# The MLP of a decoder layer on one core: single tiles regrouped, and weight sums stored ahead

## The chip, the core and the metric

The kernel runs on one core of one Trainium2 chip. The metric is the device time of one execution in microseconds. A core has five engines that matter here: TensorE for matrix products (its weight loads are shown apart, as PEld, since they overlap the products), VectorE (DVE), ScalarE (ACT), GpSimd (POOL), and SyncE (SP), which here issues the DMA transfers. Each engine works through its own list of instructions in order and waits at an instruction until what that instruction needs is there.

## The reference

One step of a decoder layer with 1032 tokens (a prompt of 1024 and 8 single sample tokens): an input projection, two head groups, an output projection with a layer norm, and then the MLP, which is all that the change touches:

```python
h = jnp.square(jax.nn.relu(jnp.einsum('btd,df->btf', x, w_ff1)))
x = layernorm(DN_ALPHA * x + jnp.einsum('btf,fd->btd', h, w_ff2), ln2_g, ln2_b)
```

D_MODEL is 1024 and the inner width 4096, all in f32. In tiles of 128, the first product makes 32 row tiles of h out of 8 tiles of x; the second makes 8 row tiles of the result, and its sum runs over the 32 tiles of h.

## The kernel before

**Layout and precision.** Tokens are columns: 1032 of them, in two halves of HN = 516, each in two chunks of CH = 258. An f32 operand is split (`split`, L109) into a high part, which ACT makes by a copy (L111), and a low part, which DVE or POOL makes by a subtraction (L112). Each product is then three matmuls: high by high, high by low, low by high. `product` (L1434, the matmul is L1440) runs these over the tiles of the sum, with two matmuls of 128x258 for each, one per chunk, into one PSUM buffer `sb` of two banks; there are four such buffers.

**Pairs.** Both products save matmuls where two output tiles (or two tiles of the sum) are taken together as a pair. The weights of a pair are a block of 2 x 2, A11, A12, A21 and A22, and the two halves of the tokens are the other side. Seven block products, named B21, T1, B11, B22, T2, T3 and T4, take the place of eight. Four of them need sums of the weights: s1 = A21 + A22, s2 = s1 - A11, s4 = A12 - s2 and s3 = A11 - A21. B21 uses A12, T1 uses s1, B11 uses A11, B22 uses s4, T2 uses s2, T3 uses s3 and T4 uses A22. The sides that belong to the tokens ("forms") need sums likewise.

**Where the order comes from.** In the first MLP product, and in what comes before it, TensorE's instructions run in the order in which the program gives them (L1315 sets that for this engine). Everything else, and all of the second product, is put in order by the compiler, which may move an instruction ahead of others. Buffers are another matter: a tile is asked for under a tag with a fixed number of buffers, and the buffers of one tag are handed out in the order in which the program asks for them, each one when the tile that held it before has been read for the last time.

**The first product.** Six of the 32 output tiles (PLAIN, L26: 0, 1, 14, 15, 28, 29) are made singly in an earlier stage (`plain`, L1410). The other 26 are made as 13 pairs in `ff1` (L1541). `pair` (L1455) asks for two tiles of tag `wpair`, which has four buffers of 128x1024 (512 KB), and loads them (L1460): the first holds A11 and A12, the second A21 and A22. The sums go to `wraw` (L1464 to L1467, two buffers; s1 and s4 on DVE, s2 and s3 on POOL). Results are taken out of PSUM into tiles `hst` (four buffers): an addition of two products on DVE (L1483), relu and square on ACT (L1480, L1484, L1485), and a store of h to memory (`hd`, L1486). `minus` (L1489) makes four sums of these outputs per pair, which are forms of the second product, in tiles of tag `hsum` (two buffers of 128x516), on DVE (L1491), and stores them to `ht` (L1492). The first, `minus(0)`, reads the relu of T2 and the result of B11, and stands right behind T2; two come behind T3 and one behind T4.

`pair` is a generator with seven stops. The loop in `ff1` runs the new pair five steps and fits the last two of the pair before it in between, so that TensorE runs B21 of the new pair, T3 of the old, T1 of the new, T4 of the old, and then B11, B22 and T2 of the new.

**The second product.** `ff2` (L1718) goes through the 32 tiles of h in groups (GROUPS, L23): a positive number is that many single tiles, a negative one that many pairs. For each group there are weights laid out by the host as that group needs them (`_layout`, L1804), and forms of h which are loaded and split in preparation (`plain_forms` L1568 with `h_load` L1558, tag `hraw`, two buffers; `pair_forms` L1577, loads L1591 into `hst`, 21 per group of three pairs). The forms live in a ring of 30 slots (RING, L25). A group of single tiles has 16 units (eight output tiles, two halves), a group of three pairs has 4 (`pair_unit`, L1638), each of seven products, of which the last two run beside the next unit. While one group is worked on, the preparation of the next is spread over its units (L1740). `pair_unit` loads the four blocks A of 128x384 (192 KB each) into tag `w2raw`, which has six buffers (WB, L1646), makes s1 to s4 in `wraw` (L1651, on DVE or POOL by the table WE), splits them, and adds each product to the accumulator on DVE (L1668). Where a group of pairs follows a group of single tiles, all its forms go into fresh slots; where it follows pairs, 12 of the 21 can only be made when the old group's slots come free.

The last group (four single tiles) is done by `dense_g` (L1707) together with the closing layer norm (L1773).

Of the kernel before, what the change touches and what calls it, by code (L numbers as in the profile page):

```python
# [9 lines left out]
F32 = mybir.dt.float32  # L10
F32R = mybir.dt.float32r
AF = mybir.ActivationFunctionType
OP = mybir.AluOpType
# [6 lines left out]
LBLK = [(0, 256), (768, 264), (256, 256), (512, 256)]  # L20
PBLK = [(0, 384), (384, 384), (768, 264)]
HN, CH = 516, 258
GROUPS = [2, -3, -3, 2, -3, -3, 4]  # L23
FIRST = [sum(abs(x) * (1 if x > 0 else 2) for x in GROUPS[:g]) for g in range(len(GROUPS))]
RING = "XXLLLLLLQBQBQBQBQBQBQBQQCQCQQB"  # L25
PLAIN = (0, 1, 14, 15, 28, 29)  # L26
PAIRS = [p for p in range(16) if 2 * p not in PLAIN]
FORMS = {"B11": "QL", "B21": "QL", "B12": "XX", "B22": "CL", "T1": "BQ", "T2": "BQ", "T3": "BQ", "T4": "BQ"}
TO = 2
TP = ((1, 3), (0, 1, 3), (0,), (2,))  # L30
LA = (384,384,384,256)
HE = {"B21": 0, "T1": 0, "B11": 0, "B22": 1, "T2": 1, "T3": 0, "T4": 1}
WE = (1, 0, 1, 0, 0, 0, 1, 1, 0, 1, 0)
# [26 lines left out]
class Kernel:  # L60
# [1307 lines left out]
    def out2(self, mixo, acc):  # L1368
        nc = self.nc
        V, G = nc.vector, nc.gpsimd  # L1370
        self.fm = {}
        self.hd = self.dp.tile([32, 128, NT], F32, name="hd", tag="hd")
        self.ht = self.dp.tile([14, 4, 128, HN], F32, name="ht", tag="ht")
        ws = self.resident(self.a["wout"][0], [self.x1slot("wr", w) for w in "LLLLLLBB"], self.tp)

        def units(c0):
            for n_ in range(8):
                ps = self.mmps(CH)
                yield from self.dense_q(ws[n_], mixo, c0, CH, ps)
                V.tensor_tensor(acc[n_][:, c0:c0 + CH], acc[n_][:, c0:c0 + CH], ps, op=OP.add)  # L1380
                yield 3 * CH / 2400.0

        def norm(c, half, fill):
            put = (self.form("B11", c) + self.form("B21", c)) if not half else (self.form("B12", c) + self.form("B22", c))
            for wait in self.layer_norm_x1(acc, HN * half + CH * c, CH, put, LW[2 * c + half]):
                self.ahead(fill, wait)

        order = [(0, 0), (0, 1), (1, 0), (1, 1)]
        us = [units(HN * half + CH * c) for c, half in order]
        self.ahead(us[0], 99)  # L1390
        chain = lambda *gs: (x for g in gs for x in g)
        norm(0, 0, chain(us[1], us[2]))
        self.ahead(us[1], 99)
        norm(0, 1, chain(us[2], us[3]))
        self.ahead(us[2], 99)
        if TO == 0:
            self.t_forms(acc, 0)
        first = self.plain(0)
        norm(1, 0, chain(us[3], first))
        self.ahead(us[3], 99)  # L1400
        if TO == 1:
            self.t_forms(acc, 0)
        norm(1, 1, first)
        if TO == 2:
            self.t_forms(acc, 0)
        self.t_forms(acc, 1)
        self.ahead(first, 999)
        self.ahead(self.plain(1), 999)
# [46 lines left out]
    def pair(self, p):  # L1455
# [82 lines left out]
            out(f + 1, 0, P, m4)  # L1538
        yield

    def ff1(self):  # L1541
        self.ps_ctx.close()
        self.ps_ctx = ExitStack()
        self.sb = self.ps_ctx.enter_context(
            self.tc.tile_pool(name="sb", bufs=4, space=PSUM, reuse_waits="tile"))
        prev = iter(())
        for p in PAIRS:
            cur = self.pair(p)
            for i in range(5):
                next(cur)  # L1550
                if i < 2:
                    next(prev, None)
            prev = cur
        for _ in prev:
            pass
# [12 lines left out]
    def plain_forms(self, g, out):  # L1568
        nc = self.nc
        for j in range(GROUPS[g]):  # L1570
            raw = self.h_load(FIRST[g] + j)
# [5 lines left out]
    def pair_forms(self, g, out):  # L1577
        n = -GROUPS[g]
        slots = {}
        once = GROUPS[g - 1] > 0  # L1580
        early, late = ("B21", "T1", "B11"), ("B22", "T2", "T3", "T4")
# [39 lines left out]
    def plain_units(self, g, hs, acc):  # L1621
        V = self.nc.vector
        nth = sum(1 for x in GROUPS[:g] if x > 0)
        for n_ in range(8):
# [13 lines left out]
    def pair_unit(self, g, q, fs, acc):  # L1638
        nc = self.nc
        V, G = nc.vector, nc.gpsimd  # L1640
        E = lambda i: (V, G)[i]
        n = -128 * GROUPS[g]
        A = {}
        for j in (1, 2, 3, 0):
            A[j] = self.tp.tile([128, 384], F32, name="w2raw", tag="w2raw", bufs=WB)[:, :n]
            nc.sync.dma_start(A[j], self.a["wff2_%d" % g][q][:, n * j:n * j + n])  # L1646
        A11, A12, A21, A22 = (A[j] for j in range(4))

        def add(x, y, op, eng):
            z = self.wp.tile([128, 512], F32, name="wraw", tag="wraw", bufs=2)[:, :n]  # L1650
            eng.tensor_tensor(z, x, y, op=op)  # L1651
            return z
# [18 lines left out]
        product(Q, "B21", A12, E(WE[0]), True, True)  # L1671
        out(0, 0, Q)
        yield
        s1 = add(A21, A22, OP.add, E(WE[1]))
        s2 = add(s1, A11, OP.subtract, E(WE[2]))
        T = self.bank()
        product(T, "T1", s1, E(WE[3]), True)
        out(1, 1, T)
# [2 lines left out]
        product(P, "B11", A11, E(WE[4]), True)  # L1681
        out(0, 0, P)
        yield
        s4 = add(A12, s2, OP.subtract, E(WE[5]))
        product(T, "B22", s4, E(WE[6]), False, True)
        out(0, 1, T)
        yield
        product(P, "T2", s2, E(WE[7]), False)
        out(0, 1, P)
        yield  # L1690
        s3 = add(A11, A21, OP.subtract, E(WE[8]))
        product(P, "T3", s3, E(WE[9]), False)
        out(1, 1, P)
        yield
# [204 lines left out]
```

## Time and profile before

| what | before |
|---|---|
| time, median of 3 runs | 1279.5 us (1277.76 to 1281.45) |
| profiled execution | 1279.77 us |
| its span, first to last instruction | 1278.0 us |
| PE busy | 1215.0 us, 95% of the span, 9268 matmuls |
| PEld busy | 1183.8 us, 93% |
| DVE busy | 844.6 us, 66% |
| ACT busy | 638.7 us, 50% |
| POOL busy | 513.4 us, 40% |
| mean granted clock of TensorE | 0.975 |

The profiled execution is 1.8 us longer than its span, which runs from the first to the last instruction. Busy times are sums over the instructions of an engine; engines overlap, so they don't add up to the span. The granted clock is TensorE's share of its full speed. In the views below, windows give for a stretch (from:to in us of the span) its length and the busy time and count of PE, PEld, DVE, ACT and POOL, then the granted clock, the mean busy share of the 16 DMA engines and GB/s. A line of the timeline gives the start, the duration in us, engine, line and operation, with the tile written and the tiles read (out<-in); a bracket at its end holds the idle time before it and what ended it. SPq is SP's queue of DMA issues; a DMA's duration in the chain is its time from issue to landing.

### The profile page before, as it was taken

Reading aid. Unit: us, or ns where it says so; the run is one execution under the profiler, and the core shown is the slowest. Engines: PE = TensorE matmul, PEld = TensorE weight load, DVE = VectorE, ACT = ScalarE, POOL = GpSimd, SP = SyncE. Lnnn points to the kernel's source line nnn. Section 1 sums busy time; section 2 is a strip of 40 time slices with the busy share of each in tenths; the row PEclk is TensorE's granted clock in tenths of the full one; section 3 lists DMA queues with packets and bytes.
Section 4 is the critical chain, followed back from the end, with each engine's and each line's share of the span. In section 5 each row is a group of like instructions: output and inputs, shape, how many; then the busy total and the mean of one; then the engine's idle time right before and its main releaser. Section 6 shows DMA issues by size and latency. Waiting matters only on the chain.

```text
span 1278.0 us, 25175 instructions
## 1 busy us (share of the span) xinstructions
PE 1215.0 (95%) x9268; PEld 1183.8 (93%) x9268; DVE 844.6 (66%) x1744; ACT 638.7 (50%) x1458; POOL 513.4 (40%) x540
## 2 busy tenths in 40 slices
PE   8999999899899999989999999999999999999996
PEld 7999999889899889989899999999988999989995
DVE  6477787788726885888644444444877768586577
ACT  5376676763556741377655555555544343252210
POOL 6242332362114761454423333233456543374134
PEclk9999999999979899999999999999999999999998
DMA  7323222123431262024434444445754445152112
GB/s 208 108 78 84 68 72 82 37 71 100 128 108 48 75 209 68 1 67 120 145 133 174 141 166 158 143 165 187 231 166 144 130 133 164 58 158 74 62 42 92
DMA packets 110075, 147.02 MB, mean 115 GB/s; under 512 B 30312, under 2 KB 65528, under 8 KB 109952
## 3 DMA queue, kind: packets, MB, share of 16 engines
q1 hardware_dynamic: 109952, 145.41, 36.4%
q8 instruction: 73, 1.20, 0.4%
q14 instruction: 50, 0.41, 0.1%
HBM read 100.31 MB, written 43.88 MB: 113 GB/s over the span
## 4 chain that ended last, share of the span: by engine, by line
PE 70%; DVE 15%; DMA 6%; issue 4%; ACT 3%; POOL 1%; SPq 1%; POOLq 0%; DVEq 0%; ACTq 0%
PE sb L1440 35%; PE mm L154 7%; PE mm L156 7%; PE mm L155 7%; DMA hst<-ht 2%; DVE t L112 1%; PE mm L1714 1%; DVE wlo L112 1%; PE mm L1716 1%; DMA hst<-hd 1%; PE mm L1715 1%; DVE acc L1138 1%; DVE xB L1152 1%; DVE cx L303 1%; DVE uq L376 1%
## 5 line engine op out<-in xcount | busy, mean ns | idle before, releaser
L112 POOL TENSOR_TENSOR wlo<-wraw,whi 128x512 fp32r<-128x512 f32 (+1 forms) x103 | 128.4, 1248 | 201.1 <-ACT whi L111 162.4
L111 ACT ACTIVATE whi<-wraw 128x512 fp32r<-128x512 f32 (+2 forms) x194 | 112.8, 583 | 167.9 <-PE sb L1440 107.2
L1440 PE MATMUL sb<-t,whi 128*128 128x258 f32 x1008 | 165.1, 287 | 5.7 <-ACT whi L111 4.1
L1440 PEld LDWEIGHTS sb<-t,whi 128*128 128x128 f32 x1008 | 140.7, 192 | 7.4 <-ACT whi L111 4.9
L1440 PE MATMUL sb<-xT,whi 128*128 128x258 f32 x832 | 133.8, 283 | 0.0
L154 PE MATMUL mm<-xhi,whi 128*128 128x344 f32 x384 | 126.4, 329 | 3.0 <-DVE zt L321 2.4
L156 PE MATMUL mm<-xhi,wlo 128*128 128x344 f32 x384 | 123.8, 322 | 0.0
L155 PE MATMUL mm<-xlo,whi 128*128 128x344 f32 x384 | 123.8, 322 | 0.0
L1440 PEld LDWEIGHTS sb<-xT,whi 128*128 128x128 f32 x832 | 114.3, 189 | 0.0
L1668 DVE TENSOR_TENSOR acc<-acc,sb 128x516 f32<-128x516 f32 x112 | 75.9, 686 | 53.4 <-PE sb L1440 53.2
L1440 PE MATMUL sb<-t,wlo 128*128 128x258 f32 x504 | 101.7, 287 | 3.6 <-DVE wlo L112 3.5
L1440 PE MATMUL sb<-xB,whi 128*128 128x258 f32 x624 | 100.3, 283 | 0.0
L112 DVE TENSOR_TENSOR wlo<-wraw,whi 128x512 fp32r<-128x512 f32 (+2 forms) x91 | 67.0, 739 | 41.7 <-ACT whi L111 41.6
L1440 PEld LDWEIGHTS sb<-xB,whi 128*128 128x128 f32 x624 | 85.9, 190 | 0.0
L1440 PE MATMUL sb<-xT,wlo 128*128 128x258 f32 x416 | 83.7, 283 | 0.0
L1440 PEld LDWEIGHTS sb<-t,wlo 128*128 128x128 f32 x504 | 79.0, 193 | 4.2 <-DVE wlo L112 4.2
L111 ACT ACTIVATE t<-hst 128x516 fp32r<-128x516 f32 x84 | 52.6, 632 | 52.2 <-DMA hst<-ht 26.7
L154 PEld LDWEIGHTS mm<-xhi,whi 128*128 128x128 f32 x384 | 72.3, 188 | 5.2 <-DVE zt L321 3.5
L155 PEld LDWEIGHTS mm<-xlo,whi 128*128 128x128 f32 x384 | 72.3, 188 | 0.4 <-issue 0.4
L156 PEld LDWEIGHTS mm<-xhi,wlo 128*128 128x128 f32 x384 | 72.2, 188 | 0.4 <-issue 0.4
L112 POOL TENSOR_TENSOR t<-hst,t 128x516 fp32r<-128x516 f32 x36 | 52.2, 1460 | 37.1 <-ACT t L111 36.9
L1483 DVE TENSOR_TENSOR hst<-sb,hst 128x516 f32<-128x516 f32 x40 | 27.6, 691 | 59.4 <-PE sb L1440 59.4
(513 smaller groups left out, 3549.5 us busy)
## 6 DMA issues: line engine op xcount, KB each, us to landing
hd<-hst SPq DMA_DIRECT2D x52, 258.0 KB
wpair<-in_wff SPq DMA_DIRECT2D x26, 512.0 KB
ht<-hsum SPq DMA_DIRECT2D x48, 258.0 KB
hst<-ht SPq DMA_DIRECT2D x48, 258.0 KB
w2raw<-in_wff SPq DMA_DIRECT2D x64, 192.0 KB
wraw<-in_win SPq DMA_DIRECT2D x40, 256.0 KB
hst<-hd SPq DMA_DIRECT2D x36, 258.0 KB
wraw<-in_wff SPq DMA_DIRECT2D x24, 256.0 KB
```

Of the source, the lines that this page charges most:

```text
L111: nc.scalar.activation(hi, src, AF.Copy)
L112: (lo_eng or nc.vector).tensor_tensor(lo, src, hi.bitcast(F32), op=OP.subtract)
L154: nc.tensor.matmul(ps, hi[:, k % 4, :], mh, start=(k == 0), stop=False)
L155: nc.tensor.matmul(ps, hi[:, k % 4, :], ml, start=False, stop=False)
L156: nc.tensor.matmul(ps, lo[:, k % 4, :], mh, start=False, stop=(k == last))
L303: nc.vector.scalar_tensor_tensor(out, raw[:, j:j + NP], cw[:, t, j:j + 1], out, op0=OP.mult, op1=OP.add)
L376: V.scalar_tensor_tensor(u[:, cc], ps[cc // 2][:, cc % 2], self.s2[:, hc:hc + 1], dt[:, cc, None, :].to_broadcast([128, 2, 128]), op0=OP.m ...
L1138: V.scalar_tensor_tensor(x, x, self.lnp[:, 0, i:i + 1], rb, op0=OP.mult, op1=OP.mult)
L1152: nc.vector.scalar_tensor_tensor(lo, x, b, hi.bitcast(F32), op0=OP.add, op1=OP.subtract)
L1440: self.nc.tensor.matmul(ps[:, 512 * c:512 * c + CH], a[:, k, :], forms[c][k][b], start=(start and k == 0 and a is hi and b == 0), stop=(st ...
L1483: V.tensor_tensor(h3, self.banks(ps), h3, op=OP.add)
L1668: V.tensor_tensor(a, a, self.banks(ps), op=OP.add)
```

## The change

Six tiles are still made singly in the first product, but others: 0 to 3, 28 and 29. In the second product the first group is four single tiles, then come four groups of three pairs, and four single tiles end it. The middle group of two single tiles is gone, so there are six groups for seven.

The weight sums s1 to s4 of seven of the 16 units of pairs, the first and last unit of each group of pairs (but not the last of the last group), are made in the first product: behind the five steps of each of the first seven pairs, `weight_sums` loads the unit's four blocks as two tiles of tag `wpair`, makes the four sums on DVE in tiles of tag `hsum` and stores them to a new scratch array `wd` in memory. In the second product those seven units load seven tiles (A12, s1, A11, s4, s2, s3, A22, in this order) under tag `w2raw` where the others load four, and make no sums. The other nine units are as before.

```diff
--- before.py
+++ after.py
@@ -20,12 +20,13 @@
 LBLK = [(0, 256), (768, 264), (256, 256), (512, 256)]
 PBLK = [(0, 384), (384, 384), (768, 264)]
 HN, CH = 516, 258
-GROUPS = [2, -3, -3, 2, -3, -3, 4]
+GROUPS = [4, -3, -3, -3, -3, 4]
 FIRST = [sum(abs(x) * (1 if x > 0 else 2) for x in GROUPS[:g]) for g in range(len(GROUPS))]
 RING = "XXLLLLLLQBQBQBQBQBQBQBQQCQCQQB"
-PLAIN = (0, 1, 14, 15, 28, 29)
+PLAIN = (0, 1, 2, 3, 28, 29)
 PAIRS = [p for p in range(16) if 2 * p not in PLAIN]
 FORMS = {"B11": "QL", "B21": "QL", "B12": "XX", "B22": "CL", "T1": "BQ", "T2": "BQ", "T3": "BQ", "T4": "BQ"}
+STORED = [(g, q) for g in range(1, 5) for q in (0, 3) if (g, q) != (4, 3)]
 TO = 2
 TP = ((1, 3), (0, 1, 3), (0,), (2,))
 LA = (384,384,384,256)
@@ -1370,6 +1371,7 @@
         V, G = nc.vector, nc.gpsimd
         self.fm = {}
         self.hd = self.dp.tile([32, 128, NT], F32, name="hd", tag="hd")
+        self.wd = self.dp.tile([len(STORED), 4, 128, 384], F32, name="wd", tag="wd")
         self.ht = self.dp.tile([14, 4, 128, HN], F32, name="ht", tag="ht")
         ws = self.resident(self.a["wout"][0], [self.x1slot("wr", w) for w in "LLLLLLBB"], self.tp)
 
@@ -1538,18 +1540,43 @@
             out(f + 1, 0, P, m4)
         yield
 
+    def weight_sums(self, i):
+        nc = self.nc
+        V = nc.vector
+        g, q = STORED[i]
+        n = -128 * GROUPS[g]
+        z = []
+        for j in range(2):
+            t = self.pp.tile([128, 1024], F32, name="wpair", tag="wpair", bufs=4)
+            nc.sync.dma_start(t[:, :2 * n], self.a["wff2_%d" % g][q][:, 2 * n * j:2 * n * j + 2 * n])
+            z += [t[:, 0:n], t[:, n:2 * n]]
+        A11, A12, A21, A22 = z
+
+        def put(k, x, y, op):
+            r = self.pp.tile([128, HN], F32, name="hsum", tag="hsum", bufs=2)[:, :n]
+            V.tensor_tensor(r, x, y, op=op)
+            nc.sync.dma_start(self.wd[i, k][:, :n], r)
+            return r
+
+        s1 = put(0, A21, A22, OP.add)
+        s2 = put(1, s1, A11, OP.subtract)
+        put(3, A12, s2, OP.subtract)
+        put(2, A11, A21, OP.subtract)
+
     def ff1(self):
         self.ps_ctx.close()
         self.ps_ctx = ExitStack()
         self.sb = self.ps_ctx.enter_context(
             self.tc.tile_pool(name="sb", bufs=4, space=PSUM, reuse_waits="tile"))
         prev = iter(())
-        for p in PAIRS:
+        for n_, p in enumerate(PAIRS):
             cur = self.pair(p)
             for i in range(5):
                 next(cur)
                 if i < 2:
                     next(prev, None)
+            if n_ < len(STORED):
+                self.weight_sums(n_)
             prev = cur
         for _ in prev:
             pass
@@ -1641,12 +1668,16 @@
         E = lambda i: (V, G)[i]
         n = -128 * GROUPS[g]
         A = {}
-        for j in (1, 2, 3, 0):
+        stored = STORED.index((g, q)) if (g, q) in STORED else None
+        for j in (1, 4, 0, 7, 5, 6, 3) if stored is not None else (1, 2, 3, 0):
             A[j] = self.tp.tile([128, 384], F32, name="w2raw", tag="w2raw", bufs=WB)[:, :n]
-            nc.sync.dma_start(A[j], self.a["wff2_%d" % g][q][:, n * j:n * j + n])
-        A11, A12, A21, A22 = (A[j] for j in range(4))
-
-        def add(x, y, op, eng):
+            nc.sync.dma_start(A[j], self.a["wff2_%d" % g][q][:, n * j:n * j + n] if j < 4 else
+                              self.wd[stored, j - 4][:, :n])
+        A11, A12, A21, A22 = (A.get(j) for j in range(4))
+
+        def add(k, x, y, op, eng):
+            if stored is not None:
+                return A[3 + k]
             z = self.wp.tile([128, 512], F32, name="wraw", tag="wraw", bufs=2)[:, :n]
             eng.tensor_tensor(z, x, y, op=op)
             return z
@@ -1671,8 +1702,8 @@
         product(Q, "B21", A12, E(WE[0]), True, True)
         out(0, 0, Q)
         yield
-        s1 = add(A21, A22, OP.add, E(WE[1]))
-        s2 = add(s1, A11, OP.subtract, E(WE[2]))
+        s1 = add(1, A21, A22, OP.add, E(WE[1]))
+        s2 = add(2, s1, A11, OP.subtract, E(WE[2]))
         T = self.bank()
         product(T, "T1", s1, E(WE[3]), True)
         out(1, 1, T)
@@ -1681,14 +1712,14 @@
         product(P, "B11", A11, E(WE[4]), True)
         out(0, 0, P)
         yield
-        s4 = add(A12, s2, OP.subtract, E(WE[5]))
+        s4 = add(4, A12, s2, OP.subtract, E(WE[5]))
         product(T, "B22", s4, E(WE[6]), False, True)
         out(0, 1, T)
         yield
         product(P, "T2", s2, E(WE[7]), False)
         out(0, 1, P)
         yield
-        s3 = add(A11, A21, OP.subtract, E(WE[8]))
+        s3 = add(3, A11, A21, OP.subtract, E(WE[8]))
         product(P, "T3", s3, E(WE[9]), False)
         out(1, 1, P)
         yield
```

## Rows read from the trace of the kernel before

**Rows 1.** Windows, first product: stretch, us, then busy us (count) by engine

```profile
631.00:890.00 259.00, 259.00 (x2157) 259.00 (x2156) 109.85 (x164) 138.81 (x232) 83.34 (x65) 1.00 0.44 153
```

**Rows 2.** Windows, second product: stretch, us, then busy us (count) by engine

```profile
905.00:950.00 45.00, 39.96 (x316) 38.30 (x315) 39.76 (x56) 24.04 (x44) 27.28 (x21) 1.00 0.71 208
968.00:1000.00 32.00, 28.95 (x224) 28.32 (x223) 27.34 (x29) 15.92 (x28) 26.84 (x21) 0.95 0.56 177
1000.00:1038.00 38.00, 38.00 (x318) 38.00 (x318) 23.22 (x37) 10.83 (x21) 13.12 (x13) 1.00 0.29 93
1038.00:1079.00 41.00, 37.76 (x297) 36.93 (x296) 31.33 (x48) 16.79 (x33) 14.37 (x12) 0.96 0.56 170
1123.00:1163.00 40.00, 36.71 (x285) 35.77 (x284) 31.76 (x35) 17.65 (x31) 29.92 (x21) 0.96 0.50 157
1200.00:1215.00 15.00, 13.43 (x111) 13.01 (x110) 4.61 (x8) 0.00 (x0) 0.00 (x0) 1.00 0.11 36
```

**Rows 3.** Waits of PE, 965 to 1000: us, times, longest

```profile
PE sb L1440 <- DVE wlo L112: 2.0, 1, 2.0
PE sb L1440 <- ACT whi L111: 1.0, 1, 1.0
```

**Rows 4.** Timeline of PE behind that wait: start, us, line, operation

```profile
987.29 1.06 PE L1440 MATMUL sb<-t,whi 128*128 128x258 f32 x4
```

**Rows 5.** Timeline of PE: products B21 and T1 of one pair begin

```profile
867.78 0.64 PE L1440 MATMUL sb<-xB,whi 128*128 128x258 f32 x4
873.55 0.64 PE L1440 MATMUL sb<-xT,whi 128*128 128x258 f32 x4
```

**Rows 6.** Timeline of SP: the first single tile's load

```profile
882.48 0.42 SPq L1560 DMA_DIRECT2D hraw<-hd  x1
```

**Rows 7.** Timeline of ACT: its split

```profile
887.74 1.07 ACT L111 ACTIVATE h<-hraw 128x1032 fp32r<-128x1032 f32 x1 [1.53 <-DMA hraw<-hd]
```

**Rows 8.** Tile hraw, its instructions: ns min/median/max

```profile
L112 POOL TENSOR_TENSOR h<-hraw,h x4: 2409/2417/2445, 891.3 to 1155.1; 128x1032 fp32r<-128x1032 f32 x4
```

**Rows 9.** Windows, the adds of line 1651 alone: DVE, then POOL

```profile
968.00:1000.00 32.00, 6.84 (x5) 1.91 (x2) 0.95 0.56 177
```

**Rows 10.** Line 1651, its instructions: ns min/median/max

```profile
L1651 DVE TENSOR_TENSOR wraw<-w2raw x32: 544/908/2760, 911.7 to 1195.8; 128x384 f32<-128x384 f32 x32
```

**Rows 11.** Waits of SP's queue, 640 to 850, at the loads of line 1460

```profile
SPq L1460 <- POOL wraw L1466: 14.7, 10, 1.6
SPq L1460 <- POOL wlo L112: 12.5, 10, 1.4
```

**Rows 12.** Timeline of DVE around the end of a pair's T2

```profile
868.03 0.70 DVE L1483 TENSOR_TENSOR hst<-sb,hst 128x516 f32<-128x516 f32 x1 [1.78 <-PE sb L1440]
870.10 0.70 DVE L1491 TENSOR_TENSOR hsum<-hst 128x516 f32<-128x516 f32 x1
875.81 0.70 DVE L1491 TENSOR_TENSOR hsum<-hst 128x516 f32<-128x516 f32 x1 [1.37 <-ACT hst L1485]
```

**Rows 13.** Timeline of SP: two stores from hst, and a load that waits

```profile
896.90 0.85 SPq L1486 DMA_DIRECT2D hd<-hst  x2
899.62 0.32 SPq L1591 DMA_DIRECT2D hst<-hd  x1
```

**Rows 14.** Chain that ended last, 965 to 1000: two loads of 258 KB

```profile
971.57 2.69 DMA hst<-ht
977.35 3.46 DMA hst<-ht
```

**Rows 15.** Timeline of SP: the first pair's weights are loaded

```profile
623.80 0.92 SPq L1460 DMA_DIRECT2D wpair<-in_wff  x2
```

**Rows 16.** Timeline of ACT: their first split

```profile
628.26 0.63 ACT L111 ACTIVATE whi<-wpair 128x512 fp32r<-128x512 f32 x1 [1.73 <-DMA wpair<-in_wff]
```

**Rows 17.** Tile wpair, its instructions: ns min/median/max

```profile
L111 ACT ACTIVATE whi<-wpair x39: 631/633/635, 628.3 to 882.2; 128x512 fp32r<-128x512 f32 x39
L1466 DVE TENSOR_TENSOR wraw<-wpair x13: 676/679/693, 629.5 to 861.6; 128x512 f32<-128x512 f32 x13
```

## The prediction

> **What bounds the kernel now.** I read the page's head first: PE is busy 95% of the span, so time can only be won where PE stands and lost where something new makes it stand. The windows by stage come next, because that share is an average. In the first MLP product PE is busy all of 259 us [rows 1] while DVE has 109.85: everything there is hidden behind PE, and nothing in it can be won. The second product is different. A stretch inside a group does 318 matmuls in 38 us, 119.5 ns each, without idle time; the stretches around a change of group do not [rows 2]. Their length less count times 119.5 ns is what each loses: 7.2 us (905 to 950, the first single tiles to the first pairs), 5.2 (968 to 1000), 5.5 (1038 to 1079, two changes around the middle single tiles), 5.9 (1123 to 1163) and 1.7 (1200 to 1215), together 25.5 us. That is all the change can work on in the second product. The waits of PE say what is late at such a change: prepared weights, 3.0 us in the second stretch [rows 3]; the other 2.2 us of its 5.2 are the slow clock afterwards, when four matmuls take 1.06 us [rows 4] where they take 0.64 at the full clock [rows 5]. I use 2.2 us as the price of the clock behind any stop of PE of some microseconds.
>
> **The second product.** The matmuls stay the same in number: 384 on single tiles (8 x 2 x 4 x 6 in one group for twice 8 x 2 x 2 x 6), 2016 on pairs. Sixteen evictions on DVE go, off the path.
>
> *First group of four.* It runs 16 x 24 x 0.1195 = 45.9 us where the group of two ran 23, so the 21 loads and splits of the first pair forms have twice the time. I put that change at 0.5 us (bounds 0 and today's 7.2; nearer to 0, since the same loads get twice the cover).
>
> *Its start.* Four tiles go through two hraw buffers. A load takes 5.26 us to its split [rows 6, 7], the split 1.07, the second half on POOL 2.41 [rows 7, 8]: 8.7 us for the fourth tile after its buffer is free. Two tiles in hand give half a unit in each of four banks, 48 x 0.1195 = 5.7 us of PE. I take 3.0 us (bounds 0 and 8.7).
>
> *Changes from pairs to pairs.* There are three instead of two; today they cost 5.2 and 5.9. The stored sums take the adds out of the units beside them, 6.84 us of DVE and 1.91 of POOL in the second stretch [rows 9]: DVE would fall from 27.34 of 32 us to 64%, about the 61% of the stretch that loses nothing [rows 2]. Against that, each stored unit loads seven tiles of 192 KB instead of four through six buffers, 21 more loads in all, on the queue that also brings the forms. I take half of 5.5, 2.75 us each (bounds 0 and 5.5). The last change stays at 1.7.
>
> Sum: 0.5 + 3.0 + 3 x 2.75 + 1.7 = 13.5 us for 25.5, a gain of **12.0 us** (from 23.8 gained to 8.6 lost with all bounds one way).
>
> **The first product.** Here the change adds, per pair and for the first seven of thirteen, two loads of 384 KB, four adds and four stores, and they pass through buffers that the pair needs: the four of wpair and the two of hsum. By the busy shares they would be free: four adds at 0.55 us (the shortest in [rows 10]) beside 109.85 of 259 us. The order of the buffers says otherwise.
>
> wpair: pair p holds two, its two sum tiles the other two. The next pair's first tile gets the buffer that pair p's s3 add releases, its second in today's order the one that pair p's T4 split releases [rows 11]. But T4 of pair p runs behind T1 of pair p+1 on PE, and its split behind that split, and T1 of pair p+1 adds the halves of that very second tile. Today two spare buffers break the circle. With the sum tiles in them, the second tile can only get theirs, when the last of the four adds has read them.
>
> hsum: the adds ask for their buffers behind pair p's first subtraction, which reads the relu of T2. So the sums cannot be made ahead; they begin when T2 has ended and been evicted.
>
> The chain, on a pair of before: T2 ends, its eviction starts at 868.03, the subtraction runs 870.10 to 870.80 [rows 12]. The first sum takes the other buffer at once; s2 needs the subtraction's buffer, so that store must land. A store frees its buffer 2.7 us after its issue [rows 13] (2.2 if it was the second of the two), near the loads of the same size, 2.69 and 3.46 [rows 14]. So: 870.80 + 2.7 + 0.55 (s2) + 2.7 (its store; s4 fits between) + 0.55 (the last sum) = 877.3. Then the load of 512 KB: 4.46 us from issue to split [rows 15, 16], 881.8; the add 0.68 and the split 0.63 [rows 17]: T1 can start at 883.1. It starts at 873.55 now [rows 5]. **PE stands 9.5 us**, seven times (pairs two to eight), each with 2.2 us of slow clock: 7 x 11.7 = **81.9 us**. Bounds: stores of 2.2 and a load of 2.69, 6.75 us; stores of 3.46 and a load of 5.26, 11.8 us: 62.7 to 98.3 us in all.
>
> What waits behind the new waits: s2 and the last sum stand at the head of DVE for 2.7 and 2.2 us, and behind them the next two subtractions (today at 875.81 and after, [rows 12]) and the eviction of T3; their stores wait on SP, and behind these the store of T3's tile. All this is over before T1 starts, so I put it at nothing; without that stop it would cost about 2 us a pair. The stores to memory and their issue on SP are hidden likewise.
>
> Profiled execution 1279.8 + 81.9 - 12.0 = 1349.7 us; it stands 0.3 above the median of the runs, so **1349**. Its own range goes from 1279.5 + 62.7 - 23.8 = 1318 to 1279.5 + 98.3 + 8.6 = 1386.
>
> The stores and the load are the term that no row shows in the place where they will run. The rows give 2.2 to 3.5 us for 258 KB and 4.5 to 5.3 for 512 KB. The Trainium skill, page "DMA: Bandwidth & Descriptors", section "Anatomy of one DMA — SWDGE (gpsimd) path", fits a transfer as 2.0 us plus its bytes at 436 GB/s, for another issuing path than SP's; its estimate here would be 2.6 us for a subtraction's store, 2.45 for a sum's and 3.2 for the load, a stop of 7.9 us, and 1338 in place of 1349. The trace agrees on the smallest (2.69 for 258 KB) and lies above it for 512 KB.
>
> **The rivals.**
> *The sums are made ahead (not slower).* Their tiles are loaded long before and DVE has 58% of the stage free. If the adds got hsum buffers whenever they are ready, the sum tiles would be free early. The point that decides: the last of the four adds must have ended when T2 ends, since 4.46 + 0.68 + 0.63 = 5.77 us are what B21 and T3 give (867.78 to 873.55, [rows 5]). Then only the second product's gain is left: 1267.5. For it speaks DVE's idle time; against it that every hsum tile is asked for behind the subtraction. Chance 0.13.
> *Only some pairs stop.* If buffers fall better in some of them, as three of seven: 1279.5 + 35 - 12 = 1303. For it speaks that the first pair has no predecessor and the chain has slack in no other place; chance 0.08.
> *The sums do not help, and nothing stops.* The three changes keep 5.5 us, because the forms' transfers, not the adds, are late: 0.5 + 3 + 16.5 + 1.7 = 21.7, 3.8 us gained, 1275.7: at the edge of no change. The 2.69 and 3.46 us of transfer inside the chain [rows 14] speak for it. Chance 0.04.
>
> **How the numbers follow.** The forecast has 0.75. About 0.3% (3.8 us) is what a measurement of this kernel can tell from no change. Slower by more: 0.75 + 0.08 and almost nothing of the third rival, less a little for errors in the reading: 0.82. Faster by more: 0.13 and a share of the third: 0.14. Within: 0.04. The forecast's own range of 1318 to 1386 holds about 0.72; with the case of some pairs it reaches to 1290 and holds close to 8 in 10. The rivals below 1280 are left out.
>
> **What would show it.** The first product's stage takes some 340 us instead of 259, with seven stops of PE of 7 to 12 us, each ahead of a T1, the granted clock down behind each, and none from the ninth pair on. SP's queue waits at the pair's second load for a DVE add; DVE's sums come right behind the first subtraction of each pair, with a gap of about 2 us ahead of the second and the fourth. In the second product the change near 905 to 950 has gone and the three others lose under 4 us each. The forecast is wrong if the adds stand ahead of the subtraction in DVE's order, or if the second load is issued before them; it is wrong in size if stores or loads there land outside 2.2 to 3.5 and 2.7 to 5.3 us.

## The result and the profile after

The changed kernel takes 1356.3 us (median of 4, 1354.18 to 1357.86) against 1280.5 us (4 runs): a ratio of 1.059, 95% interval 1.057 to 1.062. Its profiled execution took 1357.25 us, with a span of 1355.5 us. The forecast was 1349 us, slower.

The head of its page, with each engine's busy time:

```profile
span 1355.5 us, 25222 instructions
...
PE 1227.1 (91%) x9268; PEld 1194.9 (88%) x9268; DVE 835.2 (62%) x1727; ACT 636.1 (47%) x1450; POOL 509.1 (38%) x533
```

PE is busy 91% of the span where it was 95%.

The first product runs from the first B21 to the last T4. The windows over exactly that stage, first of the kernel before, then of the changed one (columns as in [rows 1]):

```profile
631.20:894.20 263.00, 263.00 (x2190) 263.00 (x2189) 112.01 (x165) 140.86 (x235) 85.55 (x66) 1.00 0.45 156
```

```profile
633.60:980.80 347.20, 280.65 (x2187) 277.10 (x2186) 138.99 (x195) 140.31 (x237) 91.62 (x66) 0.89 0.45 152
```

The stage before is 263.0 us long and not 259: the compiler ran a few matmuls of the first single tiles ahead of the last T4 matmuls, and [rows 1] stop 4 us short for it. It has grown by **84.2 us**. The second product, from there to the end of the span, went from 383.8 to 374.7 us, a gain of **9.1**. The stages ahead are 2.4 us longer; in the fourteen profiles of this study the first product starts anywhere from 630.3 to 635.0 us, also among kernels that differ only behind it, so I put that down to no part of the change. Sum: 84.2 - 9.1 + 2.4 = 77.5 us, the difference of the spans.

PE's waits in that stage are all of one kind (waits of PE, 633 to 982: total, times, longest):

```profile
PE sb L1442 <- ACT whi L112: 66.1, 7, 10.0
```

Seven stops of 9.44 us on average, each ahead of a T1. One of them on PE's timeline:

```profile
686.95 0.40 PE L1442 MATMUL sb<-xT,wlo 128*128 128x258 f32 x2
696.57 1.23 PE L1442 MATMUL sb<-xT,whi 128*128 128x258 f32 x4 [9.22 <-ACT whi L112]
...
698.46 1.06 PE L1442 MATMUL sb<-xT,whi 128*128 128x258 f32 x4
...
700.98 0.64 PE L1442 MATMUL sb<-xT,whi 128*128 128x258 f32 x4
```

T3 ends at 687.35; T1 starts 9.2 us later, and its first groups of four take 1.23 and 1.06 us where they take 0.64 [rows 5]: the granted clock is 0.51 from 696.57 to 700.98, the lower of its two levels, and 1.00 after it. The chain of waits that ends in that T1 (start, us, what; the small pieces left out between them add up to 0.8 us, 0.32 of it SP issuing the last sum's store):

```profile
683.75 0.71 DVE hsum L1493
...
684.47 2.51 DMA ht<-hsum
...
687.10 0.57 DVE hsum L1557
...
687.69 1.83 DMA wd<-hsum
...
689.61 0.57 DVE hsum L1557
...
690.56 4.50 DMA wpair<-in_wff
...
695.16 0.70 DVE wraw L1468
...
695.89 0.64 ACT whi L112
```

These are the links of the forecast in their order: the pair's first subtraction, its store, s2 in the buffer that this frees, the store of s2, the last sum, the load of the next pair's second tile, s1 of that pair, its split. From the end of the subtraction (684.46) to T1 it is 12.1 us; the forecast had 12.3.

One link can be read in two ways. SP issues the load right behind the last sum's store:

```profile
684.94 4.14 SPq L1558 DMA_DIRECT2D wd<-hsum  x3
...
690.19 0.32 SPq L1558 DMA_DIRECT2D wd<-hsum  x1
690.56 0.45 SPq L1462 DMA_DIRECT2D wpair<-in_wff  x1
```

So the load may have waited for a wpair buffer that the last sum frees, as forecast, or only for its turn behind stores that wait for the sums. That pairs do take buffers which sum tiles free shows in the run in_place below, where one of their loads (L1462) waits 0.4 us for the landing of a store out of a sum tile (waits of SP's queue, 640 to 860). For the changed kernel the trace doesn't separate the two readings, and no run does.

In the second product, windows of the stretches (from the first unit on; the third, fifth and seventh hold a change from pairs to pairs):

```profile
980.70:1027.70 47.00, 46.55 (x384) 45.93 (x383) 29.92 (x42) 24.65 (x41) 18.85 (x13) 1.00 0.79 254
1027.70:1055.70 28.00, 28.00 (x234) 28.00 (x234) 18.14 (x31) 9.39 (x18) 9.56 (x9) 1.00 0.45 132
1055.70:1115.70 60.00, 56.51 (x456) 56.10 (x455) 37.97 (x52) 25.05 (x46) 28.86 (x25) 0.97 0.54 162
1115.70:1130.70 15.00, 15.00 (x127) 15.00 (x126) 7.98 (x12) 3.68 (x7) 5.06 (x5) 1.00 0.17 50
1130.70:1180.70 50.00, 47.08 (x382) 46.02 (x381) 34.32 (x46) 22.33 (x43) 27.30 (x22) 1.00 0.61 184
...
1195.70:1245.70 50.00, 47.06 (x375) 46.44 (x374) 31.73 (x40) 22.13 (x38) 32.98 (x24) 0.97 0.54 164
...
1285.70:1300.70 15.00, 14.22 (x121) 14.01 (x120) 6.25 (x12) 0.00 (x0) 0.00 (x0) 1.00 0.00 0
```

Length less count times 119.5 ns [rows 2] gives what each stretch loses: 1.1 us at the start, nothing at the first change to pairs, then 5.5, 4.4 and 5.2 us at the three changes from pairs to pairs, 0.5 at the last change.

### The profile page after: what moved, and what is told of

The parts are those of the page before. It is cut to its first block, busy times and chain, and to the rows that moved or that the text cites. A ratio compares the mean times of both kernels' runs of the same rounds, so it can differ in the third digit from the quotient of the medians.

```text
span 1355.5 us, 25222 instructions
## 1 busy us (share of the span) xinstructions
PE 1227.1 (91%) x9268; PEld 1194.9 (88%) x9268; DVE 835.2 (62%) x1727; ACT 636.1 (47%) x1450; POOL 509.1 (38%) x533
## 4 chain that ended last, share of the span: by engine, by line
PE 36%; DMA 8%; DVE 4%; ACT 2%; issue 1%; POOL 1%; SPq 0%; POOLq 0%; DVEq 0%; ACTq 0%
PE sb L1442 32%; DMA wpair<-in_wff 2%; DMA hst<-ht 2%; DMA ht<-hsum 1%; PE mm L1745 1%; PE mm L1747 1%; PE mm L1746 1%; DVE wlo L113 1%; DMA wd<-hsum 1%; DMA hst<-hd 1%; DVE t L113 1%; DVE hsum L1557 1%; PE ps L1810 0%; ACT t L112 0%; ACT whi L112 0%
## 5 line engine op out<-in xcount | busy, mean ns | idle before, releaser
L1442 PE MATMUL sb<-xT,whi 128*128 128x258 f32 x832 | 145.3, 300 | 66.1 <-ACT whi L112 66.1
L112 ACT ACTIVATE whi<-wraw 128x512 fp32r<-128x512 f32 (+1 forms) x164 | 100.1, 610 | 202.5 <-PE sb L1442 109.7
L1442 PEld LDWEIGHTS sb<-xT,whi 128*128 128x128 f32 x832 | 125.0, 207 | 67.6 <-ACT whi L112 67.6
L113 POOL TENSOR_TENSOR wlo<-wraw,whi 128x512 fp32r<-128x512 f32 (+1 forms) x88 | 111.2, 1266 | 183.2 <-ACT whi L112 162.5
L113 DVE TENSOR_TENSOR wlo<-wraw,whi 128x512 fp32r<-128x512 f32 (+1 forms) x76 | 61.7, 812 | 62.2 <-ACT whi L112 62.1
L1442 PE MATMUL sb<-xT,wlo 128*128 128x258 f32 x416 | 89.5, 299 | 0.5
L1468 POOL TENSOR_TENSOR wraw<-wraw,wpair 128x512 f32<-128x512 f32 x13 | 16.7, 1283 | 182.4 <-DVE wraw L1468 156.4
L1442 PEld LDWEIGHTS sb<-xT,wlo 128*128 128x128 f32 x416 | 69.1, 203 | 2.5 <-DVE wlo L113 2.5
```

The costliest lines, as they stand in the source:

```text
L112: nc.scalar.activation(hi, src, AF.Copy)
L113: (lo_eng or nc.vector).tensor_tensor(lo, src, hi.bitcast(F32), op=OP.subtract)
L1442: self.nc.tensor.matmul(ps[:, 512 * c:512 * c + CH], a[:, k, :], forms[c][k][b], start=(start and k == 0 and a is hi and b == 0), stop=(st ...
L1468: eng.tensor_tensor(sums[name], x, y, op=op)
```

## The experiments

Each run is compared with runs of the kernel before on the same chip; the stage lengths are from its profile, with the first product and the second product (to the end of the span) cut as above.

| run | median us | ratio to before (95%) | first product | second product |
|---|---|---|---|---|
| the change | 1356.3 | 1.057 to 1.062 | 347.2 | 374.7 |
| groups_only | 1272.4 | 0.991 to 0.995 | 262.6 | 375.2 |
| three_stored | 1308.6 | 1.019 to 1.024 | 298.0 | 374.2 |
| one_step | 1293.6 | 1.007 to 1.013 | 282.4 | 375.1 |
| in_place | 1279.8 | 0.998 to 1.002 | 271.3 | 375.4 |
| ask_after | 1298.9 | 1.013 to 1.017 | 290.7 | 376.1 |
| in_place_after | 1276.7 | 0.996 to 0.999 | 266.6 | 373.7 |
| no_adds | 1273.2 | 0.993 to 0.997 | 262.7 | 373.8 |
| six_loads | 1266.4 | 0.987 to 0.991 | 262.8 | 367.7 |
| prep_later | 1274.6 | 0.994 to 0.997 | 262.7 | 378.2 |
| prep_sooner | 1275.0 | 0.995 to 0.998 | 262.6 | 373.7 |
| six_sums | 1268.6 | 0.990 to 0.993 | 266.8 | 363.0 |
| six_old | 1274.0 | 0.994 to 0.998 | 263.0 | 376.9 |

A profile is one execution, and the stage lengths are its own. For prep_sooner, six_sums and three_stored it is also the fastest one (1270.2, 1265.1 and 1306.5 us: 4.8, 3.5 and 2.1 under the medians), for prep_later the slowest (1277.0, 2.4 above).

### The groups alone, and three stored units in place of seven

groups_only, on the changed kernel:

```diff
-STORED = [(g, q) for g in range(1, 5) for q in (0, 3) if (g, q) != (4, 3)]
+STORED = []
```

> The new groups and single tiles, with no stored sums at all: every unit makes its own sums again and the first product gets nothing added. If the stops come from the sums in the first product, that stage is back at about 259.5 us (347.1 with the change) and PE waits for no weights in it. For the second product (387.4 us before, 374.9 with the change) there are two theories. Regrouping does it all: about 375 us and a time of 1280 - 12 = 1268. The stored sums do a part, as the forecast had it (2.5 to 2.9 us for each of three changes of group): about 383 us and a time near 1276. If the 2.3 us that the stages ahead of the first product have grown by belong to the choice of single tiles, 2.3 us more in either case.

three_stored:

```diff
-STORED = [(g, q) for g in range(1, 5) for q in (0, 3) if (g, q) != (4, 3)]
+STORED = [(g, q) for g in range(1, 5) for q in (0, 3) if (g, q) != (4, 3)][:3]
```

> The change with the first three of its seven stored units only, at its own place. If each set of sums costs its own stop, there are three stops of 9.4 us and the first product takes 259.5 + 3 x 12.5 = 297 us; the time is 1356 - 4 x 12.5 = 1306, plus what the second product loses at the two later changes of group whose sums aren't stored (0 if regrouping does all, about 3 to 4 us if the sums matter).

Without stored sums the first product is back at 262.6 us, with no wait of PE in it, and the kernel is faster than before. (The expectation had 387.4 us for the second product before, from a cut 4 us too early; by the cut used here it is 383.8, and the 8.6 us gained there fit the measured time.) With three sets of sums there are three stops (waits of PE, 632 to 931):

```profile
PE sb L1442 <- ACT whi L112: 27.2, 3, 9.2
```

The stage grows by 298.0 - 262.6 = 35.4 us, 11.8 a set; with seven, 84.6 / 7 = 12.1. So each set of sums brings its own stop. And the second product takes as long with no stored sums, with three sets or with seven: the gain there is the regrouping's.

### When the sums may be made

one_step moves the call by one step of the pair, ahead of the first subtraction:

```diff
                 if i < 2:
                     next(prev, None)
-            if n_ < len(STORED):
-                self.weight_sums(n_)
+                if i == 3 and n_ < len(STORED):
+                    self.weight_sums(n_)
```

> All that the change does, but the weight sums are asked for behind the fourth step of a pair instead of the fifth, so ahead of the pair's first subtraction in the program and free of T2. If the stops come from the order in which hsum's buffers are handed out, the sums are made some 6 us and more earlier, the second tile of the next pair is loaded in time, the first product takes 259.5 us (up to 265 where a stop of a microsecond is left) and the time is 1356 - 87 = about 1269. If instead the transfers that were added (2 loads of 384 KB and 4 stores a pair on SP's queue) are what comes late, the stops stay within a microsecond or two of 9.4 us each and the time stays above 1340.

in_place leaves the call where it was and takes hsum out:

```diff
-        def put(k, x, y, op):
-            r = self.pp.tile([128, HN], F32, name="hsum", tag="hsum", bufs=2)[:, :n]
-            V.tensor_tensor(r, x, y, op=op)
-            nc.sync.dma_start(self.wd[i, k][:, :n], r)
...
+        def put(k, z, x, y, op):
+            V.tensor_tensor(z, x, y, op=op)
+            nc.sync.dma_start(self.wd[i, k][:, :n], z)
+        put(0, A22, A21, A22, OP.add)
+        put(2, A21, A11, A21, OP.subtract)
+        put(1, A11, A22, A11, OP.subtract)
+        put(3, A12, A12, A11, OP.subtract)
```

> All that the change does, called at the same place, but each sum is written over a block of its own tile that is no longer read (s1 over A22, s3 over A21, s2 over A11, s4 over A12), so no hsum buffer is asked for. The sum tiles still take the two spare wpair buffers, and now until their stores have landed. By the theory of hsum's order the sums are made as soon as their tiles are loaded, the stops go, the first product takes 259.5 to 265 us and the time is about 1269. If the two spare wpair buffers alone were enough to stop PE, whatever the sums wait for, the stops stay at 5 to 10 us each and the time is 1315 to 1356.

Both take the stops down, by 64.8 and 75.9 us of the stage, with all of the added transfers still there: it is not the transfers. But neither comes to 262.6, nor within the 259.5 to 265 us and the time of about 1269 that I had expected of each. In one_step the sums no longer wait for T2, but they stand behind the third and fourth subtraction of the pair before, which needs that pair's T4. DVE there:

```profile
709.29 0.70 DVE L1493 TENSOR_TENSOR hsum<-hst,hsum 128x516 f32<-128x516 f32 x1 [3.16 <-ACT hst L1487]
710.02 0.56 DVE L1557 TENSOR_TENSOR hsum<-wpair 128x384 f32<-128x384 f32 x1
...
713.62 0.56 DVE L1557 TENSOR_TENSOR hsum<-hsum,wpair 128x384 f32<-128x384 f32 x1 [0.93 <-DMA ht<-hsum]
...
716.18 0.56 DVE L1557 TENSOR_TENSOR hsum<-wpair 128x384 f32<-128x384 f32 x1 [0.81 <-DMA wd<-hsum]
...
721.86 0.69 DVE L1468 TENSOR_TENSOR wraw<-wpair 128x512 f32<-128x512 f32 x1 [2.45 <-DMA wpair<-in_wff]
```

The first sum starts when hsum is free of that subtraction (709.99), the last ends at 716.74, then the load, and s1 of the next pair at 721.86: the old chain, begun earlier in the pair. T1 stands 1.3 to 2.7 us for it, five times; all waits of PE come to 12.1 of the 19.8 us over 262.6.

In in_place no sum waits for hsum, and T1's operands are there. What is left are waits for an eviction of PSUM, at the first pair above all. DVE's timeline, then PE's:

```profile
644.33 0.69 DVE L1468 TENSOR_TENSOR wraw<-wpair 128x512 f32<-128x512 f32 x1 [6.56 <-DMA wpair<-in_wff]
644.94 0.69 DVE L1485 TENSOR_TENSOR hst<-sb,hst 128x516 f32<-128x516 f32 x1
```

```profile
645.68 1.17 PE L1442 MATMUL sb<-xT,whi 128*128 128x258 f32 x4 [2.01 <-DVE hst L1485]
...
647.08 1.06 PE L1442 MATMUL sb<-xT,whi 128*128 128x258 f32 x4
```

DVE stands 6.56 us at s1 of the next pair, whose tile has not landed, and the eviction that PE needs is behind it in DVE's order. It is done at 645.6, and PE starts. The other three waits for an eviction, of 0.5 to 1.2 us, are of this kind: 1.8 to 3.3 us of DVE at a load or at a store from hsum, with the eviction further back. The four make 4.6 of the 8.7 us over 262.6; the slow clock after the first (1.17 and 1.06 us for four matmuls; granted clock 0.53 from 645.68 to 649.30) is part of the rest. After the other three the granted clock stays at 1.00.

### Asked for a pair later

ask_after, on the changed kernel; in_place_after is the same move on in_place:

```diff
-            if n_ < len(STORED):
-                self.weight_sums(n_)
...
+                if i == 1 and 0 < n_ <= len(STORED):
+                    self.weight_sums(n_ - 1)
```

> All that the change does, with the same tiles and buffers, but the weight sums of a pair are asked for one pair later, behind the first two steps of the next pair. The next pair's two weight tiles then take the two spare wpair buffers, and the sum tiles those that the old pair frees. The sums come later than in the change (their second tile waits for the old pair's T4), so a theory in which late sums or the added transfers stop PE leaves stops like those of the change, 9 us seven times. By the theory of the circle (second tile of the next pair, last sum, T2) nothing that T1 needs waits for a sum any more: the stops go, the first product takes 262.6 us as with the groups alone, up to 270 with small waits, and the time is 1272 to 1280.

> Both moves together: sums written over blocks that are no longer read, and asked for behind the first two steps of the next pair. Neither hsum's order nor the next pair's weights hang on a sum. The small waits of the run with sums in place (DVE standing at a weight sum or at the next pair's s1 with an eviction of PSUM behind it, 8.7 us in the first product with what the clock adds) should be gone or move to other places: first product 262.6 to 266 us, time 1272 to 1276, the same as the groups alone, since the stored sums have so far shown no gain in the second product (374.7 us with them, 375.2 without).

My expectation for ask_after was wrong. The stage takes 290.7 us, with stops of 0.8 to 2.9 us at seven T1. I had thought that nothing T1 needs would hang on a sum once the next pair's tiles are asked for first. But four tiles are still asked for per pair, two for the pair and two for sums in turn, and there are four buffers: the second tile of the pair after that is loaded only behind the last sum. SP, and DVE beside it:

```profile
711.17 2.67 SPq L1558 DMA_DIRECT2D wd<-hsum  x2
713.90 0.42 SPq L1462 DMA_DIRECT2D wpair<-in_wff  x1
```

```profile
705.45 0.74 DVE L1493 TENSOR_TENSOR hsum<-hst,hsum 128x516 f32<-128x516 f32 x1 [3.07 <-ACT hst L1487]
706.22 0.56 DVE L1557 TENSOR_TENSOR hsum<-wpair 128x384 f32<-128x384 f32 x1
...
712.94 0.56 DVE L1557 TENSOR_TENSOR hsum<-wpair 128x384 f32<-128x384 f32 x1 [1.49 <-DMA wd<-hsum]
...
719.70 0.69 DVE L1468 TENSOR_TENSOR wraw<-wpair 128x512 f32<-128x512 f32 x1 [3.53 <-DMA wpair<-in_wff]
```

The load at 713.90 follows the store of the sum that ends at 713.50, and the sums follow the subtraction of 705.45, as in one_step. So asking for the next pair's tiles first doesn't help; when the sums may be made is what counts. In one_step and ask_after they stand behind the same subtraction, and the stops at T1 are of one size (1.3 to 2.7 and 0.8 to 2.9 us); behind the first subtraction, in the changed kernel, they are 9.0 to 10.0. in_place_after, with no hsum and the call later, brings the stage to 266.6 us, of which 1.6 us are waits for an eviction. The other 2.4 us over 262.6 I have not traced; the granted clock is 1.00 there, so it isn't the clock. The time is 1276.7, still above that of the groups alone; stage and time are just outside what I had expected (to 266 and 1276).

### What is late at a change of group

no_adds, on groups_only, keeps the list of the seven units beside a change of group, without `weight_sums` and with the four plain loads in each; it leaves out their sums, and the products take plain blocks of the weights in their place:

```diff
-                return A[3 + k]
+                return A[(2, 0, 2, 1)[k - 1]]
```

> The new groups with nothing stored, in which the seven units beside a change of group load four tiles and make no sums at all: their products take plain blocks of the weights in place of s1 to s4, so 28 adds of the second product are left out. It bounds from above what taking the sums away can gain there, with no extra loads. By the forecast's working (half of 5.5 us at each of three changes) the second product falls from the 375.2 us of the groups alone to about 367 and the time is 1264. If forms, not weight sums, are what comes late, it stays within 2 us of 375 and the time is 1270 to 1273.

With 28 adds gone and no load added it takes 1273.2 us, the time of groups_only: the adds that the change stores away were not what the changes of group wait for. The changed kernel shows what else is late. ACT at the second product's first change from pairs to pairs, and DVE behind it; PE waits there 1.85 us for the first and 1.63 us for the second:

```profile
1085.72 0.63 ACT L112 ACTIVATE t<-hst 128x516 fp32r<-128x516 f32 x1 [1.25 <-DMA hst<-ht]
1086.26 0.51 ACT L112 ACTIVATE whi<-w2raw 128x384 fp32r<-128x384 f32 x1
```

```profile
1086.38 1.21 DVE L113 TENSOR_TENSOR t<-hst,t 128x516 fp32r<-128x516 f32 x1 [3.33 <-ACT t L112]
1087.52 1.63 DVE L113 TENSOR_TENSOR wlo<-w2raw,whi 128x384 fp32r<-128x384 f32 x1
...
1089.67 0.55 DVE L113 TENSOR_TENSOR wlo<-w2raw,whi 128x384 fp32r<-128x384 f32 x1
```

The weight's split (1086.26) stands in ACT's order behind the split of a form (1085.72) that waits for its load, and on DVE likewise. The second of PE's two waits isn't the load's alone: the subtraction at 1087.52, at whose end PE goes on, takes 1.63 us, and one of the same shape 0.55 at 1089.67 (see the last section). To test the loads I gave the forms more buffers. six_loads, on groups_only, with a counter `fn` in `pair_forms`:

```diff
-            raw = self.hst()
+            self.fn += 1
+            raw = self.tp.tile([128, NT], F32, name="hraw", tag="hraw", bufs=2)[:, :HN] if self.fn % 3 == 0 else self.hst()
```

> The new groups with nothing stored, and every third form of a pair is loaded into one of the two hraw buffers (idle between the first and the last group) instead of hst, so six form loads can be under way instead of four. At a change of group today ACT's split of a weight block stands behind the split of a form whose load has not landed (1.25 us at 1085.72 in the changed kernel). If the loads' lead is what is short, those waits go: of the 14.5 us that the three changes lose, 4 to 8 us, second product 367 to 371 us, time 1265 to 1268. If the slots of the ring or the work of the splits themselves (ACT, DVE and POOL in that stretch) set the pace, the second product stays within 2 us of 375 and the time at 1271 to 1274.

It is the fastest kernel of the study, 1266.4 us, faster than the kernel before and than groups_only. Its second product (columns as above):

```profile
972.10:1032.10 60.00, 57.96 (x478) 57.34 (x477) 46.83 (x60) 25.36 (x48) 36.06 (x29) 1.00 0.48 144
...
1047.10:1097.10 50.00, 47.48 (x380) 47.13 (x379) 39.15 (x51) 22.13 (x43) 29.62 (x25) 0.97 0.53 159
...
1112.10:1162.10 50.00, 48.97 (x404) 48.56 (x403) 38.11 (x49) 22.77 (x40) 36.04 (x27) 1.00 0.48 149
```

The three changes lose 60 - 478 x 0.1195 = 2.9, then 4.6 and 1.7 us: 9.2 in place of the change's 15.1. ACT's waits for the loads of pair forms over the second product, in groups_only and in six_loads (total, times, longest):

```profile
ACT t L112 <- DMA hst<-hd: 25.9, 18, 3.6
...
ACT t L112 <- DMA hst<-ht: 18.6, 21, 1.8
```

```profile
ACT t L112 <- DMA hraw<-hd: 10.8, 7, 2.9
...
ACT t L112 <- DMA hst<-ht: 7.0, 6, 1.7
...
ACT t L112 <- DMA hraw<-ht: 3.0, 2, 1.8
...
ACT t L112 <- DMA hst<-hd: 0.9, 2, 0.7
```

They have fallen from 44.5 to 21.7 us. The forms of single tiles also go through hraw, and for their loads ACT waits longer than in groups_only, where it was 2.4 us:

```profile
ACT h L112 <- DMA hraw<-hd: 11.1, 5, 3.6
```

Two runs moved the preparation in the program instead (on groups_only, FDE's last number from 4 to 0 and to 8):

> The new groups with nothing stored, and the preparation of the next group spread over all 20 steps of a group of pairs instead of the first 16. If forms come too late at a change, this makes it worse: 5 us or more in all, 1277 or above. If the compiler's order and the free slots decide and not the place in the program, within 2 us of 1272.

> The same, spread over the first 12 of the 20 steps. The nine forms that have a free slot are then made sooner; the twelve others wait for slots that come free in the last unit, so their splits stand longer at the head of ACT, DVE and POOL. If free slots bound the changes, no gain (1271 to 1275) or a loss of a few us; if the pace of the splits does, 2 to 5 us gained.

Both came out 2 to 3 us above groups_only, under the 0.3% that can be told from nothing. Neither the 5 us lost that prep_later had for late forms nor the 2 to 5 us gained of prep_sooner came: the place in the program is not what holds the forms up.

The last two put the form loads into the whole change (with the sums of in_place_after), and into the kernel before:

> The whole change with its sums in place and asked for behind the next pair's first two steps (1276.7 us), and every third form load into hraw. With the groups alone that took the second product from 375.2 to 367.8 us. If the stored sums were of no use only because the forms were later, they should show now: second product under 366 us, and a time under 1268 in spite of the 3 to 4 us that the first product still loses to them. If they are of no use at all, the second product stays at 366 to 369 us and the time is 1269 to 1271, above the 1266.4 of the groups with form loads alone.

> The kernel before with its seven groups, and only the form loads changed: every third form of a pair into hraw, which the middle group of two single tiles uses as well. If the gain of 6 us belongs to the form loads and not to the new groups, about 1274 (280 less 6). If hraw's use by the middle single tiles puts their loads in the way of the forms, 1277 to 1282.

six_old gains 0.2 to 0.6% without any regrouping, so the two gains add up: 5.1 us from the loads there, 7.9 from the groups in groups_only, 13.5 from both in six_loads (differences of medians). six_sums is not faster than six_loads (0.990 to 0.993 beside 0.987 to 0.991). Its profile shows a shorter second product, 363.0 us, and a first one that is 4 us longer; with a time of 1268.6 it fits neither of the two outcomes that I had set against each other. Whether stored sums save a few us once the forms are on time stays open: that profile is the run's fastest, and the saving is no larger than what the sums cost in the first product.

## Why the prediction was right, and where it was not

**The circle in the first product: right, with one link argued.** The order of hsum, the store waits, the load behind the last sum, seven stops, none from the ninth pair on: all as written. That the load waits for the last sum's buffer, and not for its turn on SP's queue, is the link that stays argued. A stop was put at 9.5 us and took 9.44. The terms: the store of the subtraction 2.51 us (2.7 forecast), s2's store 1.83 (2.7), the load 4.50 (4.46 to the split). So the total is closer than its terms, which is luck: the two stores are 1.06 us shorter, and the steps between, at which the forecast put nothing, take 0.8. s2's store is under the forecast's own bound of 2.2 us for a store, and the gap of DVE ahead of the fourth sum, which was to be about 2 us, is 0.88. The estimate worked out from the Trainium skill, page "DMA: Bandwidth & Descriptors", section "Anatomy of one DMA — SWDGE (gpsimd) path", came to 2.6, 2.45 and 3.2 us, from a fit for another issuing path than SP's: the trace agrees for the first, is 0.6 us shorter for the second and 1.3 us longer for the load, and the stop of 7.9 us that follows from it was not seen.

**The price of the clock: right in kind, undersized.** I took 2.2 us a stop. The stage grew by 84.2 us, of which 66.1 are waits: (84.2 - 66.1) / 7 = 2.6 us. That is 2.7 us more over the seven stops; the waits themselves came to 0.4 us less.

**"The stored sums take the adds out of the units beside them": this step failed.** The three changes were to lose 2.75 us each and lose 5.5, 4.4 and 5.2. Taking every such add away moved nothing (no_adds). I had read DVE's busy share in the stretch, and not what the late splits stood behind. The third rival, "because the forms' transfers, not the adds, are late", had this half of the story: with more buffers for those loads the three changes lose 9.2 us in six_loads, where the changed kernel loses 15.1.

**The start and the first change: too dear.** 3.0 and 0.5 us were forecast, 1.1 and 0 measured, and 0.5 for 1.7 at the last change. So the second product's gain of 12.0 us came out as 9.1: two errors of opposite sign, of which the one at the three changes is the larger.

**"I put it at nothing": true here only.** What queues behind s2 and the last sum on DVE was hidden by the stop itself, as stated. Once the stop is gone it is not: in in_place evictions that stand behind waiting work on DVE cost PE 4.6 us, and a slow clock once. SP did not stand at the load, as I had written, but at the sums' own stores ahead of it.

**The rivals.** The sums were not made ahead; one_step, in_place and in_place_after show what it would have taken, and none of them brought the 1267.5 us that the first rival named, since each kept 4 to 20 us in the first product and the sums gave nothing back in the second. All seven pairs stopped, not some.

The profiled execution was forecast at 1349.7 us and took 1357.25: 2.9 us of that are the second product's, 2.3 the first's, and 2.4 lie in the stages ahead, which vary by as much between profiles.

## What to carry to other kernels

Work that is free by busy shares can still stop the critical engine if it takes buffers of a tag that the critical path uses, or stands ahead of its loads in a queue: follow each tag in the order of the program, and ask for every tile what frees its buffer and whether that waits for the engine you want to keep busy. Before work is moved away from a stretch, look at what the late instruction stands behind in its engine's order, not at the engine's load; leaving that work out for one run tells what moving it can bring. Buffers that lie idle for most of a stage (hraw here) can lengthen the lead of loads at no cost in memory, though those for whom they were meant may wait longer.

## What the runs showed of the hardware

A split's subtraction of 128x384 on DVE that runs beside a GpSimd instruction can take three times as long: 1.63 us at 1087.52 above, with a GpSimd split from 1087.37 to 1088.73, and 0.55 us at 1089.67 with none. Over the changed kernel's groups of pairs (1028 to 1268), all 34 such subtractions without overlap took 0.54 or 0.55 us; the 11 with it took 0.55 to 1.64, median 1.06. The GpSimd split:

```profile
1087.37 1.36 POOL L113 TENSOR_TENSOR t<-hst,t 128x516 fp32r<-128x516 f32 x1 [0.33 <-ACT t L112]
```

The Trainium skill, page "SBUF — State Buffer", section "Who interferes with whom", states that a DVE instruction with two SBUF inputs contends with a GpSimd instruction that reads SBUF; these rows agree.
